# A two-layer trunk (retention, then chunked attention): the first stage rebuilt in eight steps, two output groups summed without gate, narrow products not padded

## The chip, the core and the metric

One core of a Trainium2 chip runs the whole kernel. TensorE (PE) multiplies, VectorE (DVE), ScalarE (ACT) and GpSimd (POOL) do the elementwise work, SyncE (SP) mostly issues DMA transfers. The metric is the time of one execution on the device in microseconds, as the median over several executions. Besides that, one execution was recorded by the hardware profiler; all rows below are from it.

## The reference, cut to what matters

The input x is 512 tokens by 1024, in 4-byte floats. Each of the two layers computes a modulation (shift, scale, gate; 3 x 1024 values) from the vector c, normalises x, projects it, mixes, and adds the gated result to x.

```python
cond = silu(c)
for i in range(2):
    shift, scale, gate = split(cond @ ada_w[i] + ada_b[i], 3)
    h = rms_norm(x, norm_g[i]) * (1 + scale) + shift
    out = retention(h) if i == 0 else attention(h)
    x = x + gate * out
# retention: q, k, v, g = split(h @ ret_w_in); rotary tables on q, k (4 heads of 256)
#   o = (q k^T * decay) v, causal by chunks of 64
#   out = (rms_norm(o per head) * silu(g)) @ ret_w_out
# attention: 16 heads of 128, q and k normalised, a bias per relative position,
#   softmax over all earlier chunks; out = (o * silu(g)) @ att_w_out
```

## The kernel before

All large products are made in the rounded 4-byte format F32R. To keep precision, each operand is split into a high part (rounded copy, made by ScalarE) and a low part (residual, made by VectorE), and each product is three products: high by high, high by low, low by high. A product instruction takes a stationary block of 128x128 and streams up to 512 columns. A `Chunk` is 512 columns of a projection: 8 row blocks of 128 (`kt`) in two halves of four, by four column or token blocks (units).

Layer 0 begins with a first stage (lines 342 to 398, run once). `cond`, the row c, is broadcast to 128 partitions by a 512 KB transfer, and goes through Silu. The four tiles of x (128 tokens each) are normalised (`norm_rows`: two Squares with sums on ScalarE, an addition on VectorE, two operations on GpSimd for the reciprocal root, two scalings) and transposed by TensorE into `xT`. `prepare(s)` runs four times, each for 256 rows of h: the modulation (`ada_dot`, a multiplication with a sum over 1024 values on VectorE, one for each 128 rows of scale and of shift), the scaling of h, its split, and the loads and splits of 256 rows of the weights. The products in this stage are those of the values of head 0 (`rv0`) and of half of its q and k (`rqk0_0`); the other half (`rqk0_2`) follows as a chunk of its own, then the gate projection `rg0`. The rotary tables (`cos`, `sin`) are computed behind the stage.

For each of the four heads n then come q and k, the values, the gate, and in between the scores (`scores`, tile `st`), the mix (`mix`, tile `ro`) and the output projection of an earlier head (`out_proj`, tile `po_r`). Every output weight is multiplied by the gate on GpSimd (line 219) before it is split, so a head's result can be added to x directly (line 327). In layer 1 there are 16 heads: `softmax` (tile `as`), `turn` (tile `pt`), `mix` (tile `ao`). Scores and mixes are causal: of four blocks of keys the j-th needs 512 - 128 j columns, but no product is narrower than 256 (`max(..., 256)`); the columns that this adds are zeros or are not read.

The order on each engine is set by a scheduler, from the written program and a simulated timeline. `at(u, fn)` hangs work on unit u of the sequence, so the modulation sums for the gate of layer 0 and for layer 1 (`side_load`, `side_dot`) are spread over layer 0. The tile pools set which buffer is reused: `raw`, `whi`, `wlo` (weights and their parts) have two buffers each, the pools of accumulators `pm` and `pa` four each.

Of the kernel before, what the change touches and what calls it, by code (L numbers as in the profile page):

```python
# [17 lines left out]
P = 128  # L18
# [24 lines left out]
def hybrid_trunk_kernel(  # L43
# [30 lines left out]

    cond = cp.tile([P, D], F32, name="cond")
# [3 lines left out]
    nc.gpsimd.dma_start(ng, norm_t)  # L79
    bt = cp.tile([P, 2, 24], F32, name="bt")  # L80
    nc.gpsimd.dma_start(bt, ada_bt)
# [7 lines left out]
    ident = cp.tile([P, P], F32, name="ident")  # L89
    make_identity(nc, ident)  # L90
# [4 lines left out]
    mhalf = cp.tile([P, 40], F32, name="mhalf")  # L95
    nc.gpsimd.memset(mhalf, -0.5)

    with tc.high_priority():
        nc.scalar.activation(cond, cond, AF.Silu)
# [12 lines left out]
    gates = [cp.tile([P, D], F32, name=f"gate_{i}") for i in range(2)]  # L112

# [49 lines left out]
    def norm_rows(t, tag, scalar=False):  # L163

        xn, ss = [], sp.tile([P, 2], F32, tag="ss", name=f"ss_{tag}_{t}")
        for half in range(2):
            xh = np_.tile([P, 512], F32, tag="p", name=f"xn_{tag}_{t}_{half}", bufs=6)
            nc.scalar.activation(
                xh, xs[t][:, half * 512 : (half + 1) * 512], AF.Square,
                accum_out=ss[:, half : half + 1],  # L170
            )
            xn.append(xh)
        s1 = sp.tile([P, 16], F32, tag="s1", name=f"s1_{tag}_{t}")
        nc.vector.tensor_tensor(s1[:, 0:1], ss[:, 0:1], ss[:, 1:2], ALU.add)
        rs = rstd_of(s1[:, 0:1], D, 1)
        for half in range(2):
            src = xs[t][:, half * 512 : (half + 1) * 512]
            if scalar:
                nc.scalar.activation(xn[half], src, AF.Copy, scale=rs)
            else:  # L180
                nc.vector.tensor_scalar(xn[half], src, rs, None, ALU.mult)
        return xn

# [62 lines left out]
    class Chunk:  # L246


        def __init__(self, name, w_in, cols, transposed, evac, pool=pm, tag="pm"):
# [4 lines left out]
            self.ps = []  # L254

        def load(self, half, ks=range(4), parts=None):
# [5 lines left out]
            )  # L262

# [13 lines left out]
        def units(self, halves=(0, 1), loaded=False):  # L277
            for half in halves:
                for u in range(self.n):
                    def one(half=half, u=u):  # L280
                        if u == 0 and not loaded:
                            self.load(half)
# [27 lines left out]
    def out_proj(name, w_out, row0, ys, gate, store=None, t_outer=False, done=None, rstd=None):  # L310
        ws = [None, None]

        def unit(half, t):
            csl = slice(half * 512, (half + 1) * 512)
            if ws[half] is None:
                ws[half] = load(
                    [(ALLC, w_out[row0 : row0 + 512, csl])], f"{name}_{half}", scale=gate[:, csl],
# [5 lines left out]
            if rstd is None:  # L323
                nc.vector.tensor_tensor(xs[t][:, csl], ps, xs[t][:, csl], ALU.add)
            else:
                rs = rstd()[:, t : t + 1]
# [579 lines left out]
```

## Time and profile before

| | us |
|---|---|
| median of 3 executions | 983.57 |
| lowest, highest | 983.48, 985.53 |
| profiled execution, its own time | 982.98 |
| its span, first to last instruction | 981.2 |
| TensorE busy | 949.3 |
| VectorE busy | 601.1 |
| ScalarE busy | 373.8 |
| GpSimd busy | 184.7 |

A row of the timeline gives start, duration, engine, line, operation, the tile written and the tiles read, shape, and in brackets the idle time of the engine before it with what ended it. A product's duration is its latency; the cost in a stream is the distance from start to start. The chain of work counts the same products by that distance.

### The profile page before, as it was taken

The numbers are of one execution on the slowest core, as the hardware profiler recorded it, in microseconds if no ns is written. First come the engines' busy times: TensorE is split into PE (matmuls) and PEld (weight loads), VectorE is DVE, ScalarE is ACT, GpSimd is POOL, SyncE is SP. The second block draws the span as 40 slices with busy tenths as digits, with TensorE's granted clock in tenths as the row PEclk, the third lists the DMA queues.
The fourth block names the chain that finished last, engine by engine and source line by source line (L and its number), as shares of the span: only waits on it lengthen the run. The fifth ranks groups of instructions, "written<-read, shape, count | busy, mean of one in ns | idle before, by whom it ended". The sixth has DMA issues, their size and how long they took to land.

```text
span 981.2 us, 11783 instructions
## 1 busy us (share of the span) xinstructions
PE 949.3 (97%) x4528; PEld 793.6 (81%) x4528; DVE 601.1 (61%) x1023; ACT 373.8 (38%) x785; POOL 184.7 (19%) x169
## 2 busy tenths in 40 slices
PE   3889999999999999999999999999999999999997
PEld 2778888888888888778788888888878888888886
DVE  4977796568544775864455557444676346555674
ACT  6233322232233233354444445233543244444441
POOL 3000520051002012503001250002520012004410
PEclk8899999999999999999999999999999999999999
DMA  9654436434443433312333213223212232223202
GB/s 352 241 191 160 149 99 204 151 108 140 150 150 108 150 100 104 97 57 80 101 97 97 79 62 103 91 87 96 97 58 93 87 97 90 79 70 99 95 1 86
DMA packets 70296, 111.76 MB, mean 114 GB/s; under 512 B 11888, under 2 KB 36512, under 8 KB 70240
## 3 DMA queue, kind: packets, MB, share of 16 engines
q1 hardware_dynamic: 58256, 103.29, 31.5%
q0 software_dynamic: 10832, 5.62, 2.1%
q10 hardware_dynamic: 1152, 2.10, 0.6%
q8 instruction: 35, 0.57, 0.2%
q14 instruction: 21, 0.17, 0.1%
HBM read 108.83 MB, written 2.10 MB: 113 GB/s over the span
## 4 chain that ended last, share of the span: by engine, by line
PE 86%; DMA 4%; issue 4%; DVE 3%; ACT 1%; POOL 1%; SPq 0%; POOLq 0%; ACTq 0%; DVEq 0%
PE pm_aqk L233 5%; PE pm_aqk L231 5%; PE pm_aqk L232 5%; PE po_a L231 3%; PE po_a L233 3%; PE po_a L232 3%; PE pm_av L232 3%; PE pm_av L233 3%; PE pm_rg L239 3%; PE pm_rg L240 3%; PE ao L765 3%; PE as L725 3%; PE pm_av L231 3%; PE pm_rg L241 3%; PE ro L540 3%
## 5 line engine op out<-in xcount | busy, mean ns | idle before, releaser
L231 PE MATMUL pm_aqk<-whi_aqk,hTh 128*128 128x512 f32 x256 | 102.3, 400 | 1.1 <-ACT hTh L200 1.1
L233 PE MATMUL pm_aqk<-whi_aqk,hTl 128*128 128x512 f32 x256 | 100.4, 393 | 0.0
L232 PE MATMUL pm_aqk<-wlo_aqk,hTh 128*128 128x512 f32 x256 | 100.2, 391 | 0.0
L124 DVE CUSTOM_DVE_ANT_0 ada<-ada,cond 128x1024 f32<-128x1024 f32 x48 | 63.3, 1332 | 1.7 <-DMA ada<-in_ada_t_dram 1.7
L219 POOL TENSOR_TENSOR raw_r<-raw_r,gate 128x2048 f32<-128x2048 f32 x8 | 38.2, 4771 | 106.3 <-DMA raw_r<-in_ret_w_out_dram 92.9
L231 PE MATMUL pm_rv<-whi_rv,hTh 128*128 128x512 f32 x128 | 51.2, 407 | 6.7 <-ACT hTh L306 6.7
L231 PEld LDWEIGHTS pm_aqk<-whi_aqk,hTh 128*128 128x128 f32 x256 | 48.1, 188 | 10.9 <-ACT hTh L200 1.5
L233 PEld LDWEIGHTS pm_aqk<-whi_aqk,hTl 128*128 128x128 f32 x256 | 48.1, 188 | 10.6 <-DVE hTl L201 0.4
L232 PEld LDWEIGHTS pm_aqk<-wlo_aqk,hTh 128*128 128x128 f32 x256 | 48.2, 188 | 9.2
L734 ACT ACTIVATE p<-p,nm 128x128 f32<-128x128 f32 (+1 forms) x64 | 35.9, 563 | 48.7 <-DVE nm L732 47.6
L223 DVE TENSOR_TENSOR wlo_aqk<-raw_aqk,whi_aqk 128x2048 fp32r<-128x2048 f32 x16 | 36.6, 2290 | 28.0 <-ACT whi_aqk L222 28.0
L728 DVE CUSTOM_DVE_ANT_0 p<-as,br 128x128 f32<-128x128 f32 (+1 forms) x64 | 30.4, 486 | 36.9 <-PE as L725 34.0
L241 PE MATMUL pm_rqk<-hTh,wlo_rqk 128*128 128x512 f32 x128 | 49.7, 391 | 2.5 <-DVE wlo_rqk L223 2.5
L713 POOL DMA_DIRECT2D br<-in_att_bias_dram x16 | 13.4, 839 | 204.4 <-DVE nm L732 168.8
L232 PE MATMUL pm_rv<-wlo_rv,hTh 128*128 128x512 f32 x128 | 50.9, 402 | 0.0
L239 PE MATMUL pm_ag<-hTh,whi_ag 128*128 128x512 f32 x128 | 50.7, 397 | 0.0
L240 PE MATMUL pm_ag<-hTl,whi_ag 128*128 128x512 f32 x128 | 50.5, 394 | 0.0
L231 PE MATMUL po_r<-whi_r,yh 128*128 128x512 f32 x128 | 49.8, 391 | 0.5 <-ACT whi_r L222 0.5
L241 PE MATMUL pm_ag<-hTh,wlo_ag 128*128 128x512 f32 x128 | 50.2, 395 | 0.0
L233 PE MATMUL po_r<-whi_r,yl 128*128 128x512 f32 x128 | 50.1, 392 | 0.0
L232 PE MATMUL po_r<-wlo_r,yh 128*128 128x512 f32 x128 | 50.0, 391 | 0.0
L231 PE MATMUL pm_av<-whi_av,hTh 128*128 128x512 f32 x128 | 50.0, 391 | 0.0
(199 smaller groups left out, 2548.6 us busy)
## 6 DMA issues: line engine op xcount, KB each, us to landing
ada<-in_ada_t_dram SPq DMA_DIRECT2D x32, 512.0 KB, 4.4
raw_aqk<-in_att_w_in_dram SPq DMA_DIRECT2D x32, 512.0 KB, 4.6
ada<-in_ada_t_dram SPq DMA_DIRECT2D x8, 1024.0 KB, 13.8
raw_rg<-in_ret_w_in_dram SPq DMA_DIRECT2D x8, 1024.0 KB, 5.1
raw_r<-in_ret_w_out_dram SPq DMA_DIRECT2D x8, 1024.0 KB, 5.0
raw_ag<-in_att_w_in_dram SPq DMA_DIRECT2D x8, 1024.0 KB, 5.2
raw_av<-in_att_w_in_dram SPq DMA_DIRECT2D x8, 1024.0 KB, 5.1
raw_a<-in_att_w_out_dram SPq DMA_DIRECT2D x8, 1024.0 KB, 4.9
```

The source lines that it names most:

```text
L124: return nc.vector.tensor_tensor_reduce(raw, raw, cond, 1.0, 0.0, ALU.mult, ALU.add, mod[:, layer, block : block + 1])
L219: nc.gpsimd.tensor_tensor(raw, raw, scale.unsqueeze(1).broadcast_to([P, k1 - k0, width]), ALU.mult)
L223: nc.vector.tensor_tensor(lo, raw, f32(hi), ALU.subtract)
L231: nc.tensor.matmul(ps, a_h, wh[:, k, :], start=first and k == 0, stop=False)
L232: nc.tensor.matmul(ps, a_h, wl[:, k, :], start=False, stop=False)
L233: nc.tensor.matmul(ps, a_l, wh[:, k, :], start=False, stop=last and k == 3)
L239: nc.tensor.matmul(ps, wh[:, k, csl], h, start=first and k == 0, stop=False)
L240: nc.tensor.matmul(ps, wh[:, k, csl], l, start=False, stop=False)
L241: nc.tensor.matmul(ps, wl[:, k, csl], h, start=False, stop=last and k == 3)
L540: nc.tensor.matmul(ps[:, S - w :], a[:, fsl], b[:, psl], start=j == 0 and z == 0, stop=j == 3 and z == 2,)
L728: nc.vector.tensor_tensor_reduce(p[:, :w], ps[:, :w], br[:, S - w :], 1.0, -3.0e38, ALU.add, ALU.max, mx)
L734: nc.scalar.activation(p[:, :w], p[:, :w], AF.Exp, bias=nm, accum_out=sm)
```

## The change

The first stage runs in eight steps of one row block each, and each step has all eight column blocks: the values and both halves of q and k of head 0. Its code is written instruction by instruction, and `in_order` binds every engine to the written order from there to the evacuation of the values; TensorE gets 20 products whose result nobody reads (`warm`). c comes as one row of 4 KB on the queue of ScalarE; two products with a column of ones spread it over the partitions. The rotary tables are cut into two operations a step. The weights of `rg0` are fetched and cut in the stage's last steps.

The heads 0 and 1 are now projected without the gate: head 0's result overwrites x (on ScalarE), head 1's is added, and later four side sums multiply x by the gate and add the original x, which is loaded again. The side sums are now 36, each 11/4 units apart.

Scores and mixes take products of 128 columns where only 128 are needed.

```diff
-    nc.sync.dma_start(cond, c_row.broadcast_to([P, D]))
+    nc.scalar.dma_start(cond[0:1, :], c_row)
...
+    for t in range(NT):
+        nc.sync.dma_start(xs[t], x[t * P : (t + 1) * P, :])
...
+    def rstd_of_halves(ss, tag, t):
+        ms = sp.tile([P, 2], F32, tag="s1", name=f"s1_{tag}_{t}")
+        nc.vector.tensor_scalar(ms[:, 0:1], ss[:, 0:1], 1.0 / D, EPS, ALU.mult, ALU.add)
...
+        nc.gpsimd.tensor_tensor(rs, ms[:, ss.shape[1] - 1 : ss.shape[1]], mhalf[:, 0:1], ALU.pow)
...
-                    [(ALLC, w_out[row0 : row0 + 512, csl])], f"{name}_{half}", scale=gate[:, csl],
+                    [(ALLC, w_out[row0 : row0 + 512, csl])], f"{name}_{half}",
+                    scale=gate[:, csl] if part > 1 else None,
...
+            if part == 0:
+                nc.scalar.activation(acc, ps, AF.Copy, scale=rs)
...
+        def loads(k):
+            raw[k] = st.tile([P, 2, D], F32, tag="ada", name=f"ada_0_{k}", bufs=3)
+            nc.sync.dma_start(raw[k], rows[k])
...
+            nc.sync.dma_start(rw[k][:, 0, :], ret_w_in[ksl, 2 * D : 2 * D + 512])
...
+        def warm(n):
+
+            for _ in range(n):
+                nc.tensor.matmul(
+                    idle, ones_r, ones_r.unsqueeze(1).broadcast_to([P, 4, P]), start=True, stop=True
+                )
+
+        def scale_sum(k):
+            ada_dot(raw[k][:, 1, :], 0, NK + k)
+
+        def shift_sum(k):
+            nc.vector.scalar_tensor_tensor(
+                gs[:, 0, k : k + 1], mod[:, 0, NK + k : NK + k + 1], bt1[:, k : k + 1],
+                ng[:, 0, k : k + 1], ALU.add, ALU.mult,
+            )
+            ada_dot(raw[k][:, 0, :], 0, k)
+            nc.gpsimd.tensor_tensor(
+                sh[:, 0, k : k + 1], mod[:, 0, k : k + 1], bt[:, 0, k : k + 1], ALU.add
+            )
...
+        def h_hi(k):
+            hs[k] = np_.tile([P, S], F32, tag="p", name=f"h_0_{k}", bufs=6)
+            nc.scalar.activation(
+                hs[k], xT[:, k, :], AF.Identity, bias=sh[:, 0, k : k + 1], scale=gs[:, 0, k : k + 1]
+            )
+            nc.scalar.activation(hT["h"][:, k, :], hs[k], AF.Copy)
...
+        for k in range(2, NK):
+            if k + 2 < NK:
+                loads(k + 2)
+            scale_sum(k)
+            shift_sum(k)
+            w_hi(k, 0)
+            w_hi(k, 1)
+            h_hi(k)
+            w_lo(k, 0)
+            w_lo(k, 1)
+            for _ in range(2):
+                next(rope, None)
+            h_lo(k)
+            products(k - 1, 1)
+            products(k, 0)
+            if k == 6:
+                first_g = Chunk("rg0", ret_w_in, [(ALLC, 2 * D + W2)], True, None)
+                first_g.ready = {0: first_g.fetch(0)}
+        first_g.cut(first_g.ready[0])
+        products(NK - 1, 1)
...
-                w = max(S - j * P, 256)
+                w = S - j * P
...
+            if layer is None:
+                tc.keep_in_program_order(
+                    nc.vector.tensor_tensor(xs[block], xs[block], gates[0], ALU.mult)
+                )
+                tc.keep_in_program_order(nc.vector.tensor_tensor(xs[block], xs[block], raw, ALU.add))
+                return
...
-            u = 2 + 2 * z if z < 8 else 20 + (z - 8) * 7 // 2
+            u = 4 + z * 11 // 4
```

TensorE at the start of the program, before: `hp` are the transposes of x, `pm_rv` the products of the values.

```order
L368 MATMUL hp_2_1_190<-ident,xn_2_1_174 128x128 x4
L368 MATMUL hp_3_0_209<-ident,xn_3_0_197 128x128 x4
L368 MATMUL hp_3_1_215<-ident,xn_3_1_199 128x128 x4
L231 MATMUL pm_rv_0_277<-whi_rv_0_241,hTh_111 128x512
L232 MATMUL pm_rv_0_277<-wlo_rv_0_242,hTh_111 128x512
```

And the same place after; `cp` is the spread row c, `idle` the tile that nobody reads.

```order
L551 MATMUL cp_141<-cond,ones 128x512
L484 MATMUL hp_0_0_170<-ident,xn_0_0_168 128x128 x4
L495 MATMUL idle<-ones_r 128x512 x2
L484 MATMUL hp_1_0_180<-ident,xn_1_0_178 128x128 x4
L495 MATMUL idle<-ones_r 128x512 x2
L484 MATMUL hp_2_0_201<-ident,xn_2_0_199 128x128 x4
L495 MATMUL idle<-ones_r 128x512 x2
L484 MATMUL hp_3_0_214<-ident,xn_3_0_212 128x128 x4
L495 MATMUL idle<-ones_r 128x512 x14
L541 MATMUL pm_rv_0_262<-whi_rv_0_130,hTh_118 128x512
```

Only the first half of each x tile is transposed ahead of the first products, with idle products between; the second halves stand behind the first twelve products.

VectorE inside the first stage, before, one `prepare`: `ada` and `mod` are the modulation sums, `wlo` the residuals of weights, `h` and `hTl` the scaled input and its residual.

```order
L124 ISA ada_2_258,mod<-ada_2_258,cond 128x1024
L124 ISA mod 128x1
L101 TENSOR_SCALAR kq<-qg,kg 128x1
L134 TENSOR_TENSOR mod<-mod,bt 128x2
L223 TENSOR_TENSOR wlo_rv_0_242<-raw_rv_0_240,whi_rv_0_241 128x1024
L132 TENSOR_TENSOR sh<-mod,bt 128x2
L223 TENSOR_TENSOR wlo_rqk_0_0_248<-raw_rqk_0_0_246,whi_rqk_0_0_247 128x2x256
L137 SCALAR_TENSOR_TENSOR gs<-mod,ng 128x2
L379 TENSOR_SCALAR h_2_263<-xT,gs,sh 128x512
```

And after, the whole of step 4 (`ang` is an operation of the rotary tables).

```order
L149 ISA ada_4_350,mod<-ada_4_350,cond 128x1024
L149 ISA mod 128x1
L503 SCALAR_TENSOR_TENSOR gs<-mod,bt_138,ng 128x1
L149 ISA ada_4_350,mod<-ada_4_350,cond 128x1024
L149 ISA mod 128x1
L517 TENSOR_TENSOR wlo_rv_1_133<-raw_first_352,whi_rv_1_132 128x512
L517 TENSOR_TENSOR wlo_rqk_1_137<-raw_first_352,whi_rqk_1_136 128x512
L419 SCALAR_TENSOR_TENSOR ang<-n_244,ang 128x512 x2
L527 TENSOR_TENSOR hTl_119<-h_4_446,hTh_118 128x512
```

The scaling of h has moved to ScalarE and the addition for `sh` to GpSimd; a step has half the rows and twice as many columns of q and k.

## Rows read from the trace of the kernel before

**Rows 1.** The page's head and the busy time of each engine.

```profile
span 981.2 us, 11783 instructions
...
PE 949.3 (97%) x4528; PEld 793.6 (81%) x4528; DVE 601.1 (61%) x1023; ACT 373.8 (38%) x785; POOL 184.7 (19%) x169
```

**Rows 2.** Waits of TensorE, whole span: waiting, what for, total us, times, longest.

```profile
PE hp L368 <- DVE xn L181: 9.9, 2, 9.7
PE pm_rv L231 <- ACT hTh L306: 6.7, 2, 4.0
PE hp L368 <- ACT xn L179: 2.6, 1, 2.6
PE pm_rqk L241 <- DVE wlo_rqk L223: 2.5, 1, 2.5
PE pt L745 <- DVE p L737: 2.0, 2, 1.1
...
PE po_r L231 <- ACT whi_r L222: 0.5, 1, 0.5
```

**Rows 3.** Timeline of TensorE at four marks of the first stage.

```profile
23.42 0.80 PE L231 MATMUL pm_rv<-whi_rv,hTh 128*128 128x512 f32 x1 [4.01 <-ACT hTh L306]
...
44.48 0.79 PE L231 MATMUL pm_rv<-whi_rv,hTh 128*128 128x512 f32 x1 [2.69 <-ACT hTh L306]
...
65.94 0.50 PE L241 MATMUL pm_rqk<-hTh,wlo_rqk 128*128 128x512 f32 x1 [2.52 <-DVE wlo_rqk L223]
...
76.04 0.39 PE L239 MATMUL pm_rg<-hTh,whi_rg 128*128 128x512 f32 x1
```

**Rows 4.** Stretches: us; busy of each engine (instructions); granted clock, DMA share, GB/s.

```profile
9.70:13.30 3.60, 3.37 (x15) 2.97 (x16) 2.04 (x7) 3.60 (x12) 1.79 (x4) 1.00 1.03 421
13.40:16.70 3.30, 1.16 (x11) 0.93 (x9) 3.23 (x9) 1.77 (x5) 2.58 (x2) 1.00 1.02 404
16.90:27.00 10.10, 5.79 (x17) 4.25 (x17) 7.91 (x15) 6.72 (x11) 0.00 (x0) 0.50 1.04 417
...
44.20:47.40 3.20, 2.92 (x7) 2.34 (x8) 3.20 (x7) 1.79 (x4) 0.00 (x0) 0.50 0.00 0
...
66.00:76.00 10.00, 10.00 (x44) 8.30 (x45) 9.14 (x12) 3.91 (x4) 0.00 (x0) 1.00 0.74 265
```

**Rows 5.** Timeline of ScalarE: first use of cond and of x.

```profile
5.22 1.06 ACT L99 ACTIVATE cond<-cond 128x1024 f32<-128x1024 f32 x1 [3.21 <-DMA cond<-in_c_row_dram]
6.69 0.63 ACT L168 ACTIVATE xn<-x 128x512 f32<-128x512 f32 x1 [0.42 <-DMA x<-in_x_dram]
```

**Rows 6.** Timeline of VectorE: a residual of h, then two modulation sums.

```profile
35.46 0.69 DVE L307 TENSOR_TENSOR hTl<-h,hTh 128x512 fp32r<-128x512 f32 x1
36.06 1.22 DVE L124 CUSTOM_DVE_ANT_0 ada<-ada,cond 128x1024 f32<-128x1024 f32 x1
...
37.21 1.22 DVE L124 CUSTOM_DVE_ANT_0 ada<-ada,cond 128x1024 f32<-128x1024 f32 x1
```

**Rows 7.** Timeline of GpSimd: alone, and beside a modulation sum.

```profile
8.30 0.20 POOL L117 TENSOR_SCALAR ms<-s 128x1 f32<-128x1 f32 x1 [3.52 <-DVE s L174]
...
14.97 1.42 POOL L119 TENSOR_TENSOR rs<-ms,mhalf 128x1 f32<-128x1 f32 x1
```

**Rows 8.** Groups by shape, 0 to 76 us: busy us, mean ns of one.

```profile
L443 DVE SCALAR_TENSOR_TENSOR ang<-n,ang 128x512 f32<-128x512 f32 x3 | 2.1, 684 | 0.0
...
L306 ACT ACTIVATE hTh<-h 128x512 fp32r<-128x512 f32 x8 | 4.7, 624 | 10.8 <-DVE h L379 10.8
```

**Rows 9.** Chain of work, start and us: six 256-column scores; eight transposes.

```profile
147.33 0.71 PE st L520 x6
...
457.07 0.87 PE qt L671 x8
```

**Rows 10.** Scaling by the gate (busy, mean ns); additions to x (ns minimum/median/maximum).

```profile
L219 POOL TENSOR_TENSOR raw_r<-raw_r,gate 128x2048 f32<-128x2048 f32 x8 | 38.2, 4771 | 106.3 <-DMA raw_r<-in_ret_w_out_dram 92.9 <-ACT gate L148 13.3
...
L327 DVE SCALAR_TENSOR_TENSOR x<-po_r,rs,x x32: 735/747/754, 140.7 to 439.0; 128x512 f32<-128x512 f32 x32
```

**Rows 11.** The plain 4-byte products (line 146): records, ns minimum/median/maximum.

```profile
L146 PE MATMUL gp<-diag,ones x32: 270/274/377, 100.3 to 398.8; 128*128 128x128 f32 x32
```

More of the change, by code (lines that the diff above doesn't have):

```diff
@@ L1 @@
 import math
-from contextlib import ExitStack
+from contextlib import ExitStack, contextmanager
 import numpy as np
@@ L280, in one @@
                     def one(half=half, u=u):
-                        if u == 0 and not loaded:
+                        if half in self.ready:
+                            self.w = self.ready[half]
+                        elif u == 0 and not loaded:
                             self.load(half)
@@ new lines, in hybrid_trunk_kernel @@
+        A, V = nc.scalar, nc.vector
+        acc = {}
+        cps = [pm.tile([P, 512], F32, tag="pm", name=f"cp_{half}") for half in range(2)]
+        idle = pm.tile([P, 4, P], F32, tag="pm", name="idle")
+        for half in range(2):
+            nc.tensor.matmul(
+                cps[half], ones[0:1, :], cond[0:1, half * 512 : half * 512 + 512], start=True, stop=True
+            )
+        loads(0)
+        loads(1)
+        square(0, 0, 1, A)
+        rstd_rows(0)
+        square(1, 0, 1, V)
@@ new lines, in hybrid_trunk_kernel @@
+        rstd_rows(1)
+        square(2, 0, 1, A)
+        norm(0, 0)
+        turn(0, 0)
+        keep(0, 0)
+        warm(2)
+        norm(1, 0)
+        turn(1, 0)
+        rstd_rows(2)
+        square(3, 0, 2, A)
+        square(3, 1, 2, V)
+        rstd_rows(3)
+        warm(2)
+        norm(2, 0)
+        turn(2, 0)
+        for half in range(2):
+            A.activation(cond[:, half * 512 : half * 512 + 512], cps[half], AF.Copy)
+        keep(1, 0)
+        warm(2)
+        scale_sum(0)
@@ new lines, in hybrid_trunk_kernel @@
+        norm(3, 0)
+        turn(3, 0)
+        keep(2, 0)
+        w_hi(0, 0)
+        keep(3, 0)
+        warm(14)
+        loads(2)
+        rope = rope_tables()
+        next(rope)
+        shift_sum(0)
+        h_hi(0)
+        w_lo(0, 0)
+        w_hi(1, 0)
+        scale_sum(1)
+        norm(0, 1, A)
+        norm(1, 1, A)
+        h_lo(0)
+        products(0, 0)
+        shift_sum(1)
+        h_hi(1)
+        norm(2, 1)
+        norm(3, 1)
+        w_lo(1, 0)
+        h_lo(1)
+        loads(3)
@@ L601, in hybrid_trunk_kernel @@
         blocks += [(1, b) for b in (*range(8, 16), *range(8), *range(16, 24))]
+        for t in range(NT):
+            blocks.insert(23 + 2 * t, (None, t))
         for z, (layer, block) in enumerate(blocks):
[L603 removed]
+            u = 4 + z * 11 // 4
             at(max(u - 4, 0), side_load, layer, block)
[L605 to L613 removed]
+            at(u, side_sum, layer, block)
+        with in_order():
+            ev = v_evac(0)
+            for u in range(4):
+                ev(u, acc[0, u])
+            first_g.ready[1] = first_g.fetch(1)
+            first_g.cut(first_g.ready[1])
+            for _ in rope:
+                pass
+        ev = qk_evac(0)
+        for u in range(4):
+            ev(u, acc[1, u])
+        hang_scores(0, now[0] + 4)
         for n in range(RH):
@@ L720, in softmax @@
             w = (i + 1) * P
-            w0 = max(w, 256)
+            w0 = w
             qsl = slice(i * P, (i + 1) * P)
```

310 lines of the change are left out of this document (180 added, 130 removed).

## The prediction

> **What bounds the kernel now.** I read the page first. TensorE is busy 949.3 of 981.2 us, VectorE 61%, ScalarE 38% [rows 1]: almost any time that is won must be time in which TensorE waits, or work that TensorE no longer does. Then the waits of TensorE: the first four of that list add up to 21.7 us, and all four stand in the first 66 us; those behind them are entries of 0.5 to 2.0 us, 5.9 us together [rows 2]. So the place to look at is the first stage. Its timeline has four marks: the first product of layer 0 starts at 23.42 us; then TensorE waits until 44.48 for h of the third 256 rows; it waits again for wlo_rqk until 65.94; and the first product of the gate projection (pm_rg) starts at 76.04, from where TensorE runs dense [rows 3]. The stretches by window show the granted clock: 1.00 around 13.4 to 16.7 us, then 0.50 (the level of 1.2 GHz) from 16.9 to 27 us, where TensorE had stood idle for long parts of the stretch, and 0.50 once more behind the wait at 44 us. The last window gives a price: 44 products of 512 columns in 10.00 us, 0.227 us each at the level of 2.4 GHz [rows 4].
>
> The first stage has 192 such products (values and the q, k of head 0: 8 column blocks x 8 row blocks x 3 terms). Dense they are 192 x 0.227 = 43.6 us. Before, they end at 76.04 us. What precedes and interrupts them, 32.4 us, is what the change goes after.
>
> **The change, part by part. The first stage.** The start: the queue of SyncE no longer begins with the 512 KB broadcast of cond, so a tile of x can land about when cond did; cond was used at 5.22, and the first x tile at 6.69 [rows 5]. I take 5.3, 6.6, 7.9 and 9.2 us for the four tiles, 1.26 us apart (512 KB at the 417 GB/s of rows 4), then the first pair of modulation rows (1 MB) at 11.8 to 12.1, and its weights 1.3 us later. VectorE then works in the written order: the scale sum 12.1 to 13.3 (1.15 us from start to start of such sums [rows 6]), the last half tile of x until 13.8, then the shift sum until 15.1. GpSimd's addition behind it took 0.20 us when VectorE was idle, and GpSimd's next operation 1.42 us where such a sum ran beside it [rows 7]; here VectorE has narrower work beside it, so I take 0.3. ScalarE makes h and its rounded copy in 2 x 0.62 us [rows 8]: ready at 16.7. TensorE has turned the last x tile at 14.4 and then has 14 idle products to do, 14 x 0.227 = 3.2 us at the higher level, until 17.6: the idle products, not h, end last. I start the real products at 17.7. If the clock is at its lower level there, the idle ones take 6.2 us and the start is 20.7.
>
> The clock in this place: a stretch that held nothing but transposes before it (9.7 to 13.4 us) was followed by a granted 1.00 [rows 4]. The Trainium skill, page "TensorE: Matmul & The Clock Gate", section "Part 4: PE-mode transpose", says that transposes do not count as activity for the clock; the trace speaks against it. By the row the idle products run in 3.2 us, by that page's rule only the idle ones would raise the clock and the sum would be up to 3 us longer, 973.
>
> The steps: each of the eight needs 1.5 MB, 3.8 us at 417 GB/s, so memory is faster than TensorE, whose 24 products take 5.45 us. VectorE per step: two sums (2.30), gs (0.15), two residuals of weights and one of h (3 x 0.60, from start to start [rows 6]), two operations of the rotary tables (at most 2 x 0.69 [rows 8]): 5.6 us at most, 5.2 where the table operations are short ones. The two engines are level, and TensorE enters the third step with VectorE some 1.3 us ahead (VectorE starts the third scale sum at about 24.8, and its h must be there when TensorE gets through the 60 products and the 16 second-half transposes that are queued first, at about 30). So I let TensorE set the pace and add 0.8 us for seams. The 16 transposes that stand among the products cost 0.109 us each (8 in 0.87 us [rows 9]): 1.7 us. The stage ends at 17.7 + 43.6 + 1.7 + 0.8 = 63.8 us, against 76.04: **-12.2 us**. Behind it the gate projection needs its split weights: ScalarE and VectorE do the cut right after the last h, at about 59 us, and its 1 MB is ordered some 10 us earlier, so nothing new is late there. Without that cover the price would be the 2 to 4 us of the cut.
>
> **Two groups without gate.** Four scalings on GpSimd of 4.77 us go (19 us) [rows 10]; TensorE's list of waits has no entry that ends with them but the 0.5 us on whi_r, which is at the last groups, where the scaling stays. Eight additions of 0.75 us leave VectorE [rows 10] for eight copies on ScalarE. VectorE gets eight passes over 128x1024, about 1.15 us each (the same width as the sums), 9.2 us in all, against 6.0 removed, and the queue gets 2 MB more. VectorE has over a third of layer 0 free and these passes stand some 15 to 30 units ahead of the next use of x: nothing. If a pass does get in front of an evacuation, it costs up to its 1.15 us each; I keep 1 us of that for the range.
>
> **Tiles not padded.** 168 products shrink from 256 to 128 columns (24 scores, 48 mixes in layer 0, 48 scores and 48 mixes in layer 1). A product of 256 columns takes 0.71 / 6 = 0.119 us [rows 9]. The trace has no 128-column product in this rounded format. The nearest row by shape, transposes with a load of 128 columns each, gives 0.109 us [rows 9]; there the load, not the streaming, sets the pace. That gives 168 x -0.010 = **-1.7 us**. Ends: below, the streaming alone, 0.119 - 0.054 = 0.065 us (256 columns less make 0.108 between a 512 and a 256), -9.1 us; above, products of 128 columns in plain 4-byte format, of which there are 16 in the program and 32 records in the trace [rows 11], so two passes of 0.109 each, 0.218: +16.6 us. I take 0.109, since it needs no second pass, and the 512- and 256-column products in this format show only one record each.
>
> The other edits (statistics on VectorE for one GpSimd operation less, no zero fill, tables earlier) lie beside TensorE's work: nothing. The profiled execution has 982.98 us around its span of 981.2, 0.59 below the median of 983.57. Sum: 982.98 - 12.2 - 1.7 + 0.59 = 969.7, so **970 us**.
>
> **Rivals.**
> - A narrow product costs two passes. For it: the records of the plain format [rows 11]. Against: one record per product at 256 and 512 columns. Then +16.6 stands for -1.7: 983.57 - 12.2 + 16.6 = 988, slower than before. It decides from 0.119 + 12.2 / 168 = 0.192 us a product upwards.
> - A narrow product costs its streaming only, 0.065 us: the load hides under the product before, as it does under wide ones; against it the transposes. 983.57 - 12.2 - 9.1 = 962. The Trainium skill, page "TensorE: Matmul & The Clock Gate", section "Back-to-back issue gap", gives about 81 ns for a 128-column product in a stream of loads and products; by it, as an estimate, the saving would be 168 x 38 ns = 6.4 us and the time 965. No row here shows either.
> - The written order sets a slower pace: shift sum, GpSimd, ScalarE and h's residual become one chain. Two sums and gs 2.45, GpSimd at 1.42, ScalarE 1.24, residual 0.60 and four hand-overs of about 0.1 make 6.1 us a step, 0.65 more than TensorE's 5.45, in six steps 3.9; with a start at 19.7 instead of 17.7 that is 5.9: 976. For it: engines that may no longer pass a late operation; against: VectorE's other operations of the step cover most of GpSimd's time.
> - The stage wins nothing, because the three engines wait for each other in the new order as long as they did before: 983.57 - 1.7 = 982. Against it: each wait of rows 2 has a named cause that the new order moves.
>
> **How the numbers follow.** Forecast 0.68 (966 to 974), slower pace 0.14, two passes 0.11, streaming only 0.04, nothing won 0.03. The range 964 to 980 holds the forecast with a late start, and the slower pace, about 8 in 10; it leaves out both of the extreme prices of the narrow product. A difference of 0.2%, about 2 us, is what a measurement of this kernel can tell from none. Faster by more: 0.68 + 0.14 + 0.04 = 0.86; within: 0.03; slower: 0.11.
>
> **What would show it.** The first pm_rg product near 64 us; the first real product near 18 us with the clock at 1.00 from there on; no wait of TensorE over 1 us between; a 128-column product following another after about 0.11 us (0.22 and two records: the first rival; 0.07: the second); the idle products ending after h is ready. The forecast is wrong if TensorE waits for hTl or hTh in each step, or if the later waits of 5.9 us grow because the side sums stand elsewhere in layer 0.

## The result, and the profile after

| | us |
|---|---|
| before, median of 4 executions | 983.53 |
| after, median of 4 | 970.56 (968.85 to 973.68) |
| ratio, 95% interval | 0.9867 (0.9838 to 0.9896) |
| after once more, beside the experiments, 6 executions | 973.03 (969.12 to 975.03), ratio 0.9895 (0.9869 to 0.9920) |
| profiled execution of after, its span | 969.74, 968.0 |

The change is worth 9 to 13 us by the medians, 8 to 16 by the intervals; the forecast of 970, a gain of 13.6, stands just beyond the larger of the medians. The sum behind it does not hold in the same way: one term was too large, one shows nothing in time, and one that was put at nothing turned out to keep the rest from being lost.

The page of after, its span and its busy times, which answer to [rows 1]:

```profile
span 968.0 us, 11851 instructions
PE 950.2 (98%) x4552; PEld 794.4 (82%) x4552; DVE 591.3 (61%) x1023; ACT 385.3 (40%) x800; POOL 167.1 (17%) x162
```

The waits of TensorE in after, in total us, number and longest, against [rows 2]:

```profile
PE cp L551 <- ACT cond L105: 4.1, 1, 4.1
PE hp L484 <- DVE xn L476: 3.2, 1, 3.2
PE pt L956 <- DVE p L948: 2.1, 2, 1.1
PE qt L882 <- DVE qn L874: 1.8, 1, 1.8
PE pm_rg L268 <- DVE vl L353: 1.4, 1, 1.4
PE gp L171 <- DVE diag L170: 1.1, 1, 1.1
```

The waits inside the first stage (hTh, wlo_rqk) are gone. Two stand before it (cp is the broadcast of c, hp the turning of x), and a new one stands at its end: the first gate product waits for vl, the residual of the values. The waits for p and qn stand in layer 1. The timeline of TensorE in after, around both ends of the stage:

```profile
16.54 3.44 PE L495 MATMUL idle<-ones_r 128*128 128x512 f32 x14
19.82 1.07 PE L541 MATMUL pm_rv<-whi_rv,hTh 128*128 128x512 f32 x4
...
64.39 1.07 PE L541 MATMUL pm_rqk<-hTl,whi_rqk 128*128 128x512 f32 x4
66.88 0.50 PE L268 MATMUL pm_rg<-hTh,whi_rg 128*128 128x512 f32 x1 [1.41 <-DVE vl L353]
```

The real products begin at 19.82 and run dense to 65.3; the first gate product is at 66.88 us, where [rows 3] have it at 76.04. So the stage gives 9.2 us in the profiled execution. The rest of the 13.2 us between the two profiled executions came later, and the experiments show that this rest is not the change's.

### The profile page after: what moved, and what is told of

Same layout as the page of the kernel before. It is cut to its first block, busy times and chain, and to the rows that moved or that the text cites. A ratio compares the mean times of both kernels' runs of the same rounds, so it can differ in the third digit from the quotient of the medians.

```text
span 968.0 us, 11851 instructions
## 1 busy us (share of the span) xinstructions
PE 950.2 (98%) x4552; PEld 794.4 (82%) x4552; DVE 591.3 (61%) x1023; ACT 385.3 (40%) x800; POOL 167.1 (17%) x162
## 4 chain that ended last, share of the span: by engine, by line
PE 94%; DVE 3%; DMA 1%; POOL 1%; ACT 1%; issue 1%; POOLq 0%; ACTq 0%; DVEq 0%
PE pm_aqk L260 6%; PE pm_aqk L262 6%; PE pm_aqk L261 6%; PE ro L737 3%; PE pm_rg L268 3%; PE po_a L260 3%; PE po_a L261 3%; PE po_a L262 3%; PE pm_av L260 3%; PE pm_av L261 3%; PE pm_rg L270 3%; PE pm_av L262 3%; PE pm_rg L269 3%; PE as L936 3%; PE ao L976 3%; PE po_r L260 3%
## 5 line engine op out<-in xcount | busy, mean ns | idle before, releaser
L149 DVE CUSTOM_DVE_ANT_0 ada<-ada,cond 128x1024 f32<-128x1024 f32 x48 | 60.0, 1251 | 7.6 <-DMA ada<-in_ada_t_dram 7.4
L268 PE MATMUL pm_rg<-hTh,whi_rg 128*128 128x512 f32 x128 | 50.2, 392 | 1.4 <-DVE vl L353 1.4
L874 DVE TENSOR_TENSOR qn<-pm_aqk,rs 128x512 f32<-128x512 f32 x32 | 22.0, 688 | 48.3 <-POOL rs L144 48.0
L261 PE MATMUL pm_av<-wlo_av,hTh 128*128 128x512 f32 x128 | 50.0, 391 | 0.0
L262 PE MATMUL pm_av<-whi_av,hTl 128*128 128x512 f32 x128 | 50.0, 392 | 0.0
L269 PE MATMUL pm_rg<-hTl,whi_rg 128*128 128x512 f32 x128 | 49.9, 390 | 0.0
```

Source lines behind the costliest of these rows:

```text
L149: return nc.vector.tensor_tensor_reduce(raw, raw, cond, 1.0, 0.0, ALU.mult, ALU.add, mod[:, layer, block : block + 1])
L261: nc.tensor.matmul(ps, a_h, wl[:, k, :], start=False, stop=False)
L262: nc.tensor.matmul(ps, a_l, wh[:, k, :], start=False, stop=last and k == 3)
L268: nc.tensor.matmul(ps, wh[:, k, csl], h, start=first and k == 0, stop=False)
L269: nc.tensor.matmul(ps, wh[:, k, csl], l, start=False, stop=False)
```

## The experiments

Each kernel is compared with the kernel before on the same chip. Since executions of one kernel spread over some 6 us here, the time of the first gate product is given beside each median; it differs by 0.6 us at most between the kernels that have the new stage with its start and end unchanged (66.86 to 67.45), and by 1.2 us between those that have the old one (74.96 to 76.16).

| kernel | median us | ratio to before (95%) | first gate product, us |
|---|---|---|---|
| after again | 973.03 | 0.9895 (0.9869 to 0.9920) | 67.08 |
| after, padded | 972.96 | 0.9898 (0.9875 to 0.9922) | 66.86 |
| before, not padded | 982.92 | 1.0002 (0.9990 to 1.0013) | 76.16 |
| after, no idle products | 973.55 | 0.9904 (0.9881 to 0.9928) | 69.06 |
| after, kq late | 969.44 | 0.9860 (0.9842 to 0.9879) | 66.26 |
| after, kq and bt + 1 late | 971.06 | 0.9875 (0.9848 to 0.9902) | 64.05 |
| after, gated | 991.36 | 1.0098 (1.0077 to 1.0119) | 67.45 |
| stage alone (padded, gated) | 993.92 | 1.0120 (1.0098 to 1.0142) | 67.09 |
| after, gated, row sums early | 980.95 | 0.9978 (0.9965 to 0.9992) | 67.45 |
| before, ungated | 985.77 | 1.0017 (0.9997 to 1.0037) | 74.96 |
| after, free order | 980.28 | 0.9965 (0.9945 to 0.9986) | 74.59 |
| after, both waits of the start off, values apart | 967.31 | 0.9842 (0.9816 to 0.9867) | 63.12 |

**After again.** No edit: the changed kernel beside others on one chip.

> The changed kernel itself once more, beside the other kernels of this set, as the common measure for differences of one or two microseconds: about 970.6 us, as measured before (968.9 to 973.7). Both theories on the narrow products are then judged against this run and not against one from another day.

973.03, at the upper end of what was expected; the spread is taken up in the last section.

**The narrow products: padding put back in after, taken away in before.**

```diff
-            w0 = w
+            w0 = max(w, 256)
...
-                w = S - j * P
+                w = max(S - j * P, 256)
```

> The changed kernel with its last tiles padded to 256 columns again (168 products of 128 columns become 168 of 256). Theory, from the spacing of the products in the trace of after (triples of 0.061 + 0.115 + 0.110 us against 3 x 0.119 padded): slower than after by 168 x 0.024 = 4.0 us, about 974.6 us. Rival 1, the value that the prediction took (every narrow product waits 0.109 us for its own weights): slower by 1.7 us, about 972.3. Rival 2 (a narrow product costs only its columns, 0.065 us): slower by 9.1 us, about 979.7.

> The kernel before with the padding taken away and nothing else of the change. Theory: faster than before by 4.0 us, about 979.5 us; what the narrow products save does not depend on the first stage, so it is what padding costs in the changed kernel. Rival 1 (load-paced): faster by 1.7 us, about 981.8. Rival 2 (columns only): faster by 9.1 us, about 974.4. If the two kernels differ in what the narrow products are worth by more than 1 us, the terms of the sum are not independent.

Padded, the changed kernel takes 972.96 against 973.03, with some 3 us left open either way by the intervals. The kernel before without padding takes 982.92 against 983.19, and its interval of 0.1% excludes all three of the prices that were on record (1.7, 4.0 and 9.1 us). TensorE itself does save, but less than the narrow products alone suggest. The distances from start to start of all score and mix products of at most 256 columns sum to 41.3 us in the padded kernel and to 37.8 in after, 3.5 less; the 168 narrow ones take 16.6 us, 0.099 each. The products around them get longer by some 2 us, though: all products from the first gate product to the last, with TensorE's waits taken out, take 893.1 us padded and 891.7 in after, 1.4 less, and in the two kernels with the old stage 1.5 less. A timeline of after shows the narrow ones, on one triple of the mix:

```profile
103.21 0.22 PE L737 MATMUL ro<-pth,vh 128*128 128x128 f32 x1
103.28 0.28 PE L737 MATMUL ro<-ptl,vh 128*128 128x128 f32 x1
103.39 0.27 PE L737 MATMUL ro<-pth,vl 128*128 128x128 f32 x1
103.50 0.39 PE L737 MATMUL ro<-ptl,vh 128*128 128x384 f32 x1
```

The starts are 0.07, 0.11 and 0.11 apart: the first is close to the 0.065 of the second rival, the next two to the 0.109 of the transposes. One record each, so no second pass. The waits of TensorE in the padded kernel, to be read against those of after above:

```profile
PE qt L887 <- DVE qn L879: 1.2, 1, 1.2
...
PE pt L961 <- DVE p L953: 0.9, 1, 0.9
```

pt waits 0.9 us here and 2.1 in after, qt 1.2 and 1.8, so the program takes about as long from the first gate product to the last product, 896.4 us padded and 896.8 in after. It is tempting to read this as TensorE, being sooner, standing longer before what VectorE delivers. For pt the timelines show another cause. GpSimd, then VectorE, first in after and then in the padded kernel:

```profile
566.01 4.57 POOL L248 TENSOR_TENSOR raw_a<-raw_a,gate 128x2048 f32<-128x2048 f32 x1 [2.90 <-DVE ri L947]
566.05 4.68 DVE L948 TENSOR_SCALAR p<-p,ri 128x256 f32<-128x256 f32 x1
...
566.33 4.78 POOL L248 TENSOR_TENSOR raw_a<-raw_a,gate 128x2048 f32<-128x2048 f32 x1 [2.98 <-DVE ri L952]
566.28 0.35 DVE L953 TENSOR_SCALAR p<-p,ri 128x256 f32<-128x256 f32 x1
```

In after GpSimd's scaling of a weight began 0.04 us ahead of VectorE's p, and p, 0.35 us long in the padded kernel where it began first, stood still until the scaling was done (the last section has more of these). Which of the two begins first changes from one execution of a program to the next, so this wait says nothing of the narrow products. The longer wait for qt was seen in every kernel with narrow products (1.6 to 2.3 us), but also once in a padded one (1.9, the kernel before with ungated groups); its cause was not isolated. In the kernel before without padding a new wait stands in layer 0 (timeline of TensorE), with 3.4 us at the lower clock behind it; other waits of that kernel are gone, so it is not shown to be what took the gain:

```profile
123.28 1.03 PE L157 MATMUL ss<-ident,sq 128*128 128x128 f32 x4 [3.26 <-POOL sq L545]
```

**The idle products.**

```diff
-        warm(2)
...
-        warm(14)
```

> The changed kernel without its 20 idle products; its result does not use them. Theory (the idle products lift the clock before the first real product): the first real product still starts near 19.7 us, since h is ready then and not before, but the granted clock is 0.50 for the first part of the stage and each product takes 0.43 us instead of 0.227: slower than after by 1 to 6 us, as long as the low clock lasts. Rival 1 (the 16 transposes lift the clock by themselves): the same as after within 0.5 us. Rival 2 (the idle products stand in the way, as the prediction had it): faster by up to 0.5 us and a first product a little earlier.

The kernel is whole without them, since nothing reads their result. The medians don't tell the two apart (973.55 and 973.03), the profile does. Its timeline of TensorE:

```profile
11.13 1.97 PE L484 MATMUL hp<-ident,xn 128*128 128x128 f32 x8 [3.02 <-DVE xn L476]
14.34 1.11 PE L484 MATMUL hp<-ident,xn 128*128 128x128 f32 x4 [1.24 <-DVE xn L476]
16.18 1.11 PE L484 MATMUL hp<-ident,xn 128*128 128x128 f32 x4 [0.73 <-DVE xn L476]
19.62 2.08 PE L541 MATMUL pm_rv<-whi_rv,hTh 128*128 128x512 f32 x4 [2.32 <-ACT hTh L524]
21.49 1.91 PE L541 MATMUL pm_rv<-wlo_rv,hTh 128*128 128x512 f32 x4
```

Four products take 1.87 us from start to start where after has 0.90: by this pace they run at the level of 1.2 GHz (the profile has no record of the clock ahead of 24.81 us). The first real product comes 0.2 us sooner and the first gate product 2.2 us later than in after. So the idle products do what the prediction counted on, and they stand in the way by 0.2 us at most.

**The start: kq, then kq and bt + 1.** In after, VectorE and GpSimd begin like this (timeline of either; the bracket is the idle time before):

```profile
8.65 0.21 DVE L107 TENSOR_SCALAR kq<-qg,kg 128x1 f32<-128x1 f32 x1 [7.39 <-DMA kg<-in_att_kg_t_dram]
...
10.53 1.04 DVE L476 TENSOR_SCALAR xn<-x,rs 128x512 f32<-128x512 f32 x2 [0.28 <-POOL rs L210]
...
8.21 0.25 POOL L437 TENSOR_SCALAR bt<-bt 128x8 f32<-128x8 f32 x1 [4.59 <-DMA bt<-in_ada_bt_dram]
```

kq, which only layer 1 needs, waits for the transfer of kg and stands ahead of everything in VectorE's written order; the square sum of x tile 0 had been ready since 5.66. GpSimd's bt + 1 does the same ahead of the reciprocal roots. First kq was moved alone, behind the block that is in written order:

```diff
-    kq = cp.tile([P, 1], F32, name="kq")
-    nc.vector.tensor_scalar(kq, qg, kg, float(P**-0.5), ALU.mult, ALU.mult)
...
+    kq = cp.tile([P, 1], F32, name="kq")
+    nc.vector.tensor_scalar(kq, qg, kg, float(P**-0.5), ALU.mult, ALU.mult)
     offs = (0, 512, 896, 1152)
```

> The changed kernel with one instruction moved: kq (qg times kg, needed in the second layer alone) stands behind the first stage in the written order instead of ahead of it. Theory (VectorE, which works in the written order, stood until 8.65 us waiting for the transfer of kg that kq reads, and the squares, norms and transposes of the first stage stood behind it): the first real product starts at 17.4 to 17.9 us instead of 19.82 and everything behind it comes as much sooner: faster than after by 1.9 to 2.4 us, about 968.4 us. Rival (the modulation rows or the x tiles land too late for it to matter): the first product still starts at 19.3 to 19.8 us, same time as after within 0.5 us.

The theory missed: the first real product came at 19.36 and the first gate product 0.6 us sooner. The median, 969.44, is 3.6 us below after again but 1.1 below the first set of after, and so no evidence of more. Its timeline of VectorE and GpSimd says why: the scheduler, free there, brought kq back to the front, and GpSimd still had its own wait.

```profile
9.24 0.21 DVE L632 TENSOR_SCALAR kq<-qg,kg 128x1 f32<-128x1 f32 x1 [2.20 <-DMA kg<-in_att_kg_t_dram]
...
8.83 0.25 POOL L435 TENSOR_SCALAR bt<-bt 128x8 f32<-128x8 f32 x1 [5.21 <-DMA bt<-in_ada_bt_dram]
```

Then both were moved inside the written order:

```diff
-        nc.gpsimd.tensor_scalar(bt1, bt[:, 0, NK : 2 * NK], 1.0, None, ALU.add)
...
+        nc.gpsimd.tensor_scalar(bt1, bt[:, 0, NK : 2 * NK], 1.0, None, ALU.add)
         scale_sum(0)
...
         products(NK - 1, 1)
+        V.tensor_scalar(kq, qg, kg, float(P**-0.5), ALU.mult, ALU.mult)
```

> The changed kernel with two small instructions moved off the start: kq (VectorE) behind the first stage inside the written order, and bt + 1 (GpSimd) from the head of the written order to just ahead of the first modulation row. In the run where kq alone was moved it came back to VectorE at 9.24 us and GpSimd's bt + 1 waited for its own transfer until 8.83, with the reciprocal roots behind it, and the first real product moved by only 0.46 us. Theory (both waits hold the start, either is enough): norms start near 7.6 us instead of 10.53, the first real product at 17.4 to 18.4 instead of 19.82, the idle products ending last; faster than after by 1.4 to 2.4 us. Rival (the x tiles or the modulation rows land too late): first product at 19.2 to 19.8, time as after within 0.6 us.

Timeline of VectorE, then of TensorE:

```profile
7.33 1.04 DVE L474 TENSOR_SCALAR xn<-x,rs 128x512 f32<-128x512 f32 x2 [0.28 <-POOL rs L209]
...
17.06 1.07 PE L539 MATMUL pm_rv<-whi_rv,hTh 128*128 128x512 f32 x4
...
64.05 0.50 PE L267 MATMUL pm_rg<-hTh,whi_rg 128*128 128x512 f32 x1 [1.41 <-DVE vl L352]
```

The norms begin 3.2 us sooner, the first real product comes at 17.06 and the first gate product at 64.05, 2.8 us ahead of after. The median is 2.0 us lower (971.06 against 973.03), which the spread does not let count as shown.

**Gate or no gate.** The two groups gated again, in after and in the stage alone:

```diff
-            return out_proj(f"r{n}", ret_w_out, n * 512, lambda: yy[n], gates[0], n, rstd=lambda: rstd[n], **kw)
+            return out_proj(f"r{n}", ret_w_out, n * 512, lambda: yy[n], gates[0], 3, rstd=lambda: rstd[n], **kw)
...
-        for t in range(NT):
-            blocks.insert(23 + 2 * t, (None, t))
...
-            u = 4 + z * 11 // 4
+            u = 2 + 2 * z if z < 8 else 20 + (z - 8) * 7 // 2
```

> The changed kernel with the two ungated groups of layer 0 gated again (GpSimd scales the weights of heads 0 and 1, the modulation rows spaced as in the kernel before, x not multiplied on VectorE). Theory (neither the scaling nor the row additions were on TensorE's path): same as after within 1 us. Rival (the ungated groups take part in the gain because GpSimd or VectorE delays a weight tile or a group's evacuation): slower than after by 1.5 us or more, with a wait of the layer-0 output products for a weight tile from GpSimd that is not in after's list of waits.

> The new first stage alone: the changed kernel with the last tiles padded again and the two groups gated again. Theory (the time comes from the first stage alone; the narrow products give back on waits for VectorE what they save on TensorE): faster than before by the 9.2 us that the stage saves up to the first gate product, plus what comes of later waits, 973 to 974 us. Rival (narrow products and stage add up, 4.0 and 9.2): the same 974, but then slower than after by 4.0 us, where the theory puts it at 0 to 2 us slower.

This is the largest effect of all and neither theory had its size: gated, the changed kernel takes 991.36, 18 us more than ungated and more than the kernel before; the stage alone takes 993.92. The waits of TensorE in the gated kernel:

```profile
PE po_r L260 <- ACT whi_r L251: 8.1, 1, 8.1
```

Followed back through the timelines, the 8.1 us are a late gate. The gate is made in two halves, each closed by an addition of the bias bt to its row sums. VectorE makes the first of these sums at 65.80 us in the kernel before, inside the first stage, and at 88.84 in the gated kernel. The first half has made up most of that by its end, 4.5 us late; the second half is 20 us late, its gate is evacuated at 150.32 (134.88 before), and GpSimd scales the weight behind it, after TensorE has arrived. Timelines of VectorE in the kernel before (two rows), then of VectorE, ScalarE and GpSimd in the gated one:

```profile
95.17 0.16 DVE L134 TENSOR_TENSOR mod<-mod,bt 128x4 f32<-128x4 f32 x1
122.75 0.16 DVE L134 TENSOR_TENSOR mod<-mod,bt 128x4 f32<-128x4 f32 x1
...
99.69 0.16 DVE L159 TENSOR_TENSOR mod<-mod,bt 128x4 f32<-128x4 f32 x1
143.10 0.16 DVE L159 TENSOR_TENSOR mod<-mod,bt 128x4 f32<-128x4 f32 x1
150.32 0.58 ACT L173 ACTIVATE gate<-gp 128x512 f32<-128x512 f32 x1
151.78 4.51 POOL L248 TENSOR_TENSOR raw_r<-raw_r,gate 128x2048 f32<-128x2048 f32 x1
```

The new stage brings TensorE to the output weights 9 us sooner, at 124.3 us instead of 133.1, while the sums come later. It is not for want of time on VectorE, which stands idle for 2.0 and 2.4 us ahead of that: the sums stand later in its order. Why the second half loses most is not shown. The idle stretches cost the clock as well: the granted clock is at its lower level for 17 us between 134 and 165 us of that run. Two more runs asked whether gating costs by itself or only by being late:

```diff
-            u = 2 + 2 * z if z < 8 else 20 + (z - 8) * 7 // 2
+            u = 1 + z if z < 8 else 20 + (z - 8) * 7 // 2
```

> The changed kernel with the two groups gated again, as in the run that came out near 991 us, but the first eight modulation rows summed at every unit of TensorE's work after the first stage instead of every second. Theory (there TensorE waited because the second half of the gate was ready at 150.9 us, 15 us later than in the kernel before, whose row sums VectorE could begin at 65.8 us inside the first stage): the gate comes some 20 us sooner and the wait of 8.1 us and the low clock behind it go; 971 to 979 us. Rival (GpSimd's scaling and its queue are the cost, whenever the gate comes): 985 us or more.

980.95 lies between the two, and 8 us above the ungated kernel by the ratios. The wait for whi_r is gone, with the place of the sums as the only edit, so the first run's 8.1 us were its late sums; and a wait for the gate itself has come. Timelines of TensorE, VectorE and GpSimd:

```profile
123.99 0.80 PE L171 MATMUL gp<-diag,ones 128*128 128x128 f32 x2 [7.93 <-DVE diag L170]
...
107.68 4.82 DVE L353 TENSOR_TENSOR ptl<-pf,pth 128x384 fp32r<-128x384 f32 x1
...
107.48 4.59 POOL L248 TENSOR_TENSOR raw_r<-raw_r,gate 128x2048 f32<-128x2048 f32 x1 [32.29 <-DVE mod L149]
```

TensorE reached its gate products 7.93 us before VectorE had made their operand, and VectorE had lost some 4 us of that on one residual that stood still while GpSimd scaled the weights. Around that wait the granted clock is at its lower level for 10 us (118.9 to 129.1). Lateness is one part, GpSimd's work another; how far a gated kernel could be brought by placing the sums better stays open. The other side is the kernel before with its groups ungated (the same edit of `out_proj` and of the side sums as in the change):

> The kernel before with the two groups of layer 0 summed without the gate, as in the changed kernel, and nothing else of the change. Theory (in the kernel before GpSimd's scaling is hidden, as the prediction had it, and the groups only matter once the first stage ends earlier): same as before within 1.5 us, 981 to 985 us. Rival (the scaling costs by itself, so that the two groups are a gain of their own in either kernel): faster than before by 5 us or more.

985.77 against 983.50: between 0.3 us gained and 3.6 lost by the interval. The groups without gate win nothing by themselves. What the new stage is worth with gated groups hangs on where the row sums stand: placed as in the kernel before it is 1.0% slower than that kernel, with the sums early 0.2% faster.

**The written order.** `in_order` taken out in both places:

```diff
-    with tc.tile_pool(name="st", bufs=1) as st, in_order():
+    with tc.tile_pool(name="st", bufs=1) as st:
...
-        with in_order():
+        if True:
```

> The changed kernel without the written order: the same instructions of the first stage and of the evacuations behind it, their order on each engine left to the scheduler as in the kernel before. Theory (the written order keeps VectorE's side work, the row sums of the gate and the tables of the rotation, from standing ahead of the steps; the eight steps by themselves do not): first gate product 1 to 6 us later than 66.9 us, time 971 to 976. Rival (the order does nothing, only the eight steps and the idle products do): first gate product at 66 to 67.5 us and the time of after within 1 us.

The direction was right, the size too small: the first gate product is 7.7 us later than in after and the median 7.3 us above that of after again (6.9 by the ratios, since the two come from different sets). Timeline of TensorE:

```profile
7.50 6.97 PE L495 MATMUL idle<-ones_r 128*128 128x512 f32 x17
...
21.61 3.67 PE L484 MATMUL hp<-ident,xn 128*128 128x128 f32 x16 [4.69 <-ACT xn L478]
24.93 2.05 PE L541 MATMUL pm_rv<-whi_rv,hTh 128*128 128x512 f32 x4
...
74.59 0.50 PE L268 MATMUL pm_rg<-hTh,whi_rg 128*128 128x512 f32 x1 [4.77 <-DVE vl L353]
```

The scheduler spends 17 of the 20 idle products at the very start. 16 transposes and the other three follow, then a wait of 4.69 us, and from 20.4 to 27.2 us the granted clock is at its lower level. It also turns the second half of x ahead of the first real product (which then starts at 24.93), and lets vl come late at the end.

**The best version.** Both waits of the start off, and the first value tile in two buffers of a pool that outlives the stage, since `vh` and `vl` take over the memory of the weights that the last products still read. In after the rounding of the values on ScalarE waits for those products, whose result it doesn't need (timeline of ScalarE):

```profile
65.50 2.07 ACT L352 ACTIVATE vh<-pm_rv 128x512 fp32r<-128x512 f32 x4 [4.04 <-PE pm_rqk L541]
```

The edit:

```diff
                 hi, lo = (a[:, t, :] for a in vv[n])
+                if n == t == 0:
+                    hi, lo = (np_.tile([P, 512], F32R, tag="p", name=f"{a}_0_0", bufs=6) for a in ("vh", "vl"))
```

> The changed kernel with kq and bt + 1 moved off the start, as in the run in which the first real product came at 17.06 us and the first gate product at 63.83, and besides the first tile of the values of head 0 kept in two buffers that are free by then, so that its evacuation does not wait for the last products of the stage to let go of their weights. Theory (the gap of 1.6 us at the end of the stage is that wait): first gate product at 62.4 to 62.8 us, faster than after by 3.8 to 4.5 us in the first 70 us, about 967 to 968 us in the median if the later waits stay as they are. Rival (the gap has another cause, or the next evacuations wait instead): first gate product at 63.5 us or later.

Timeline of TensorE:

```profile
17.66 1.07 PE L539 MATMUL pm_rv<-whi_rv,hTh 128*128 128x512 f32 x4
...
63.12 0.39 PE L267 MATMUL pm_rg<-hTh,whi_rg 128*128 128x512 f32 x1
```

The gap at the end of the stage is gone, so its cause is shown. The start was 0.6 us later than in the run before (VectorE had the first modulation row at 12.28 us, there at 11.65), so the first gate product is at 63.12 and not at 62.4 to 62.8; that the expectation gives 63.83 for the run before, where its trace has 64.05, makes 0.2 us of it. The median is 967.31 (965.64 to 969.68), the lowest of all and 5.7 us below after again; the two come from different sets, and the intervals of their ratios to the kernel before, 0.9816 to 0.9867 and 0.9869 to 0.9920, just miss each other.

## Why the prediction came out, step by step

The forecast was 970 and the range 964 to 980; both sets of after fall inside. By its own steps:

- **Where the start begins: 17.7 predicted, 19.82 measured.** The step that failed is "VectorE then works in the written order": the prediction followed that order from the arrival of x and did not look at what stands ahead of it, kq on VectorE and bt + 1 on GpSimd, each with a small transfer that landed only at 8.2 to 8.7 us. With both moved the start was at 17.06, and 17.66 in the best version, and the rounded h, put at 16.7 us, was ready at 16.72 in the first of these runs. The rest of that chain was right, the idle products ending last among it.
- **The pace of the steps.** TensorE sets it, as forecast: dense from 19.82 to 65.3 with the granted clock at 1.00. The rival of a slower pace did not come.
- **The end: 0.8 us of seams predicted, 1.8 measured** (66.88 - 19.82 - 43.6 - 1.7). "Nothing new is late there" was wrong: the prediction looked at the weights of the gate projection and not at the memory into which the values are evacuated. With that cured the seams were 0.2 us (63.12 - 17.66 - 45.3). Start and end together make the stage 9.2 us instead of 12.2.
- **The clock.** The idle products lift it, and no term hung on the transposes in the end. In the kernel without idle products 16 transposes with pauses of 1.24 and 0.73 us between them, and 2.32 behind them, were followed by products at the lower level; in the kernel before, transposes alone did, since their pace goes from 0.21 to 0.11 us at 13.2 us, in a stretch of transposes with one pause of 0.19 us, and the clock granted behind it is 1.00 [rows 4]. By the second (its rows stand below, timeline of TensorE), the rule of the Trainium skill ("TensorE: Matmul & The Clock Gate", "Part 4: PE-mode transpose") that transposes do not count does not hold here; the first alone would agree with it.

```profile
9.74 1.97 PE L368 MATMUL hp<-ident,xn 128*128 128x128 f32 x8 [9.74 <-DVE xn L181]
11.90 2.67 PE L368 MATMUL hp<-ident,xn 128*128 128x128 f32 x16 [0.19 <-DVE xn L181]
```

- **Groups without gate: 0 predicted.** True of the kernel before (1.0017, 0.9997 to 1.0037), and the wrong question. TensorE's waits in [rows 2] hardly show a late weight because in the old schedule the row sums for the gate begin inside the first stage and TensorE comes to the output weights 9 us later. Left gated, the changed kernel is 8 to 18 us slower than without, depending on where the row sums stand. The prediction priced this edit against the profile of before, with its cover in place, and not against its own new stage.
- **Narrow products: -1.7 predicted, none that the times show.** They take 0.099 us each, not 0.109, since one of three comes 0.07 us before the next; but the products around them take longer, and TensorE's net saving is 1.4 to 1.5 us, near the term, by parts that the prediction did not have. Neither comparison of times shows it: the one in the old kernel leaves no room for 1.0 us or more, the one in the changed kernel some 3 us either way. That TensorE saves in full what its products save was taken for granted behind the first stage; there it also waits for VectorE (5.1 us in after, 3.3 padded), and 1.1 of the 1.8 us between these is the collision of VectorE and GpSimd shown above, not the edit. Both price rivals fell, two passes by the records and streaming only by the distances.
- **The sum.** Of the 13.2 us between the profiled executions 9.2 are the stage; the remaining 4 lie in the later part, where executions spread. From first gate product to last product it took 896.8 us in the profiled execution of after and 901.4 in that of after again, for one and the same program; in before it took 900.6. The errors (start and end 3.0 too good, narrow products up to 1.7 too good) were partly made up by that: with the later set, 973.03, the time lies 3 us above the forecast, with the first set 0.6. So close a hit was luck; the stage as the main term was not.

## What to carry to other kernels

Where a written order replaces a scheduler, read each engine's list from its first instruction and ask what each one waits for: two tiny operations that each waited for a transfer cost 2.8 us, because everything stood behind them. An edit that looks worth nothing in the old profile has to be priced in the new schedule: what a change speeds up or moves may have been the cover of something else. Work saved on the busiest engine need not be time; and before a new wait is read as the effect of an edit, look whether a second execution of the same program has it too.

## What the runs showed of the hardware

That executions of one kernel spread over 6 us (969.12 to 975.03) was not expected from the times before, and a part of it can be read. VectorE's timeline in after, with GpSimd's below, and the same place in after again:

```profile
880.52 2.29 DVE L252 TENSOR_TENSOR wlo_aqk<-raw_aqk,whi_aqk 128x2048 fp32r<-128x2048 f32 x1 [1.11 <-ACT whi_aqk L251]
880.74 6.54 POOL L248 TENSOR_TENSOR raw_a<-raw_a,gate 128x2048 f32<-128x2048 f32 x1 [3.26 <-DMA raw_a<-in_att_w_out_dram]
...
882.37 6.75 DVE L252 TENSOR_TENSOR wlo_aqk<-raw_aqk,whi_aqk 128x2048 fp32r<-128x2048 f32 x1 [1.11 <-ACT whi_aqk L251]
882.36 4.61 POOL L248 TENSOR_TENSOR raw_a<-raw_a,gate 128x2048 f32<-128x2048 f32 x1 [3.46 <-DMA raw_a<-in_att_w_out_dram]
```

In after VectorE begins 0.22 us ahead of GpSimd and takes 2.29 us, and GpSimd's 4.6 us become 6.54. In after again GpSimd begins 0.01 us ahead, and VectorE's 2.29 us become 6.75. Whoever starts first runs through and the other stands still, so a fraction of a microsecond in the start decides whether GpSimd loses 1.9 us or VectorE 4.5, and for VectorE TensorE waits. The Trainium skill, page "SBUF — State Buffer", section "SBUF: two separate sides", states just this, an exclusive lock between a VectorE instruction with two inputs and GpSimd, held for the whole instruction; the trace agrees. VectorE's p at 566 us, shown with the narrow products, reads one tile and a column of scalars, and was held too.

The race can be followed further. Laid beside each other product by product, after again falls behind after by 1.5 us at 703 us, where p of 128x256 took 4.35 us beside a scaling that had begun 0.4 us earlier, and by 3.1 us between 887 and 939 us, behind the rows above: 4.6 us, all of the difference of the later part to 0.1 us. Three places of layer 1 (562 to 566, 696 to 701 and 878 to 882 us) have such a collision, and over the profiled executions of the kernels with the new stage each is won sometimes by the one engine and sometimes by the other. For the executions that were timed without a profile it was not shown that this race makes the whole spread.
